# One encoder layer on one core: rows normalised before a DMA transpose, scores in f16, a new order of the steps

## The chip, the cores and the metric

One core of one Trainium2 chip runs the whole program. The metric is the device time in microseconds (us) of that core. Of the kernel before three runs are shown: 1824.67, 1825.55 and 1826.52 us, median 1825.55 us.

## The reference, cut to what matters

The layer is computed for two sequences of 1024 rows, `x_prompt` and `x_sample`, with 1024 columns each; together 16 tiles of 128 rows.

```python
h = rms_norm(x, norm1)
proj = h @ w_in                               # 512 q, 128 k, 128 v, 512 gu, 512 gv columns
q, k = rms_norm(q, q_gain), rms_norm(k, k_gain)     # per head of 64
scores = einsum("bnqkgd,bnskd->bnkgqs", qb, kband) / sqrt(64) + bias   # bands of 3 blocks of 128
probs = exp(scores - m) / (sum(exp(scores - m)) + exp(sink - m))
a = rms_norm(probs @ vband, attn_out_gain)
g = rms_norm(gelu(gu) * (w_s @ rms_norm(gelu(gv)) + b_s), gmlp_out_gain)
x = x + concatenate([a, g]) @ w_o
h2 = rms_norm(x, norm2)
x = x + (silu(h2 @ w_gate) * (h2 @ w_up)) @ w_down
```

## The kernel before, in words

**Precision.** Nearly every product is made of three f16 products: each operand is split into a high half (the value rounded to f16) and a low half (what the rounding left out), and high x high, high x low and low x high are summed in PSUM. ScalarE makes the high half, VectorE subtracts to get the low one. For the first four tiles q, k and v are formed another way, in float32r from a transposed copy of x (`x0_load`, L800; `q0`, L854; `kv_mm`, L1089), also in halves. The scores too are three float32r products before the change: `k_hi`/`k_lo` (L1170, L1178) and `q_hi`/`q_lo` (L1174, L1183) write float32r halves, and `score_mm` (L1193) multiplies them, in pairs: the two key/value heads go to the two halves of TensorE's rows (64 each), so two products run side by side, and one step is three such pairs.

**Stages.** (1) Attention stage, roughly the first 380 us of the span: input projection, band attention, the gated branch. (2) Output projection, residual, second norm, and the transposes to `h2` (`o_product`, `h2_turn`, `h2_out`, `h2_comb`, `h2_cstore`), up to about 606 us. (3) Gate, up and down products of the FFN (`matrix`, `product` at L1824 to L1826; `down_mm` at L2318 to L2320), to the end. The pieces of h2 go to DRAM (`t_d`), come back as `tr`, and are split by `top_hi` and `top_lo` (L1726).

**Who sets the order.** The steps of stages 1 and 2 are small functions, listed by `add`. A table `WHEN` (L50) holds one number for each step, and `plan_order` sorts the steps by it; they are emitted in that order under a manual schedule, so each engine's queue (TensorE, VectorE, ScalarE, GpSimd, and SyncE's queue, which issues every DMA) runs its part of the list strictly in that order, whatever is ready. The numbers are due times: successive `q0` steps of four 128x512 products stand 90 or 91 apart. What follows the list (stage 3, from the loop over `matrix` at L2330) is ordered by the framework, and can be placed among the last listed steps.

**The path that is changed.** For a tile t from 4 on: `xn_load` (L911) brings the rows in natural layout, `xn_sum` (L913) squares and sums them on ScalarE (over the tile itself), `xn_eps` and `xn_pow` (L917, L921, the latter on GpSimd) make 1/rms. `x_load` (L924) brings the same tile transposed from a second input, `xT`. Since in that layout the scale belongs to columns, `x_diag` (L928, VectorE) puts it on a diagonal, `x_row` (L931, TensorE) multiplies that by ones to have it in every row of PSUM, and `x_scale` (L935, VectorE) multiplies. `x_hi` (L938, ScalarE) and `x_lo` (L942, VectorE) split; `x_store` (L945) keeps the halves in DRAM for the gated branch, which loads them again (`x_back`). Tiles 0 to 3 go through `x_load` to `x_store` later, for the gated branch alone. `attention` lists, for each tile and pair of heads, `score_mm`, `score_out`, `score_exp`, `p_hi`, `p_lo`, `p_turn` (L1256, a DMA that transposes the f16 halves of the exponentials) and `pv_mm`; then `o_out`, `o_sq`, `o_pow`, `o_scale` (L1297, ScalarE) and `o_store`.

**Buffers.** Tiles share tagged slots: `XL` 3, `XN` 3, `S` 9, `M` 8, `L` 12. Before, `xn` (XN) is free again after `xn_sum`, `xs` (XL) after `x_lo`, and the halves of k of one sequence take two L slots.

Of the kernel before, what the change touches and what calls it, by code (L numbers as in the profile page):

```python
# [41 lines left out]
SCALE_MAX = 1e12  # L42
LATER = (4, 5, 0, 1, 2, 3)
# [3 lines left out]
WHEN = {  # L47
    "x0_load": [
        0, 18, 30, 24, 42, 36, 1108, 1278,
    ],  # L50
    "wq_load": [
        6, 12, 494, 578, 832, 939, 1024, 1700,
    ],
    "x0_hi": [
        345, 598, 768, 683, 937, 852, 2143, 2228,
    ],
    "x0_lo": [
        427, 680, 850, 765, 1019, 934, 2225, 2310,
    ],
    "wq_hi": [  # L60
        429, 514, 1044, 1128, 1570, 1974, 2059, 2505,
    ],
    "wq_lo": [
        522, 606, 1136, 1262, 1662, 2067, 2151, 2598,
    ],
    "q0": [
        522, 639, 729, 820, 910, 1111, 1228, 1319, 1409, 1553, 1643, 1760, 1851, 1941, 2032, 2122, 2213, 2303, 2394,
        2484, 2575, 2665, 2942, 3032,
    ],
    "gram": [  # L70
        612, 1202, 1500, 1526, 1734, 2756, 2782, 2809, 2835, 2849, 2862, 2875, 2889, 2902, 2915, 2928,
    ],
    "row_load": [
        325, 409,
    ],
    "row_mm": [
        1001,
    ],
    "row_out": [
        1202,  # L80
    ],
    "row_store": [
        1447,
    ],
    "wkv_load": [
        923, 917,
    ],
    "wkv_hi": [
        2567, 2607, 1890, 1930, 1761, 1801, 1841, 1720,
    ],  # L90
    "wkv_lo": [
        2664, 2703, 1961, 2001, 1832, 1872, 1913, 1792,
    ],
    "gram_sum": [
# [12 lines left out]
        3290, 7396, 22309, 25142,
    ],
    "xn_load": [
        663, 748, 1531, 1954, 1870, 5109, 5285, 7806, 8401, 11836, 13484, 15168, 16891, 18725, 20817, 22671,  # L110
    ],
    "xn_sum": [
        1298, 1467, 2402, 2841, 2656, 5538, 5714, 8258, 9243, 12848, 14151, 15992, 17664, 19714, 21744, 23515,
    ],
    "xn_eps": [
        2812, 1610, 2546, 3009, 2800, 5701, 5866, 8471, 9414, 13000, 14338, 16140, 17826, 19893, 21888, 23692,
    ],
    "xn_pow": [
        2897, 1651, 2587, 3050, 2841, 5742, 5907, 8512, 9455, 13041, 14379, 16182, 17867, 19934, 21929, 23733,
    ],  # L120
    "kv_mm": [
        3448, 3591, 3901, 4044, 3133, 3304, 4436, 4580, 6472, 6603, 7468, 7599, 9652, 9784, 10749, 10880, 13212,
        13344, 15049, 15180, 16905, 17036, 18301, 18432, 20449, 20580, 22169, 22300, 23971, 24102, 25899, 26030,
    ],
    "q_out": [
        3216, 3159, 3274, 3331, 6459, 8377, 9536, 11750, 13192, 15033, 17178, 18991, 20785, 22549, 24298, 25909,
    ],
    "v_gain": [
        3892, 4208, 3571, 3524,
    ],  # L130
    "k_out": [
        4126, 4246, 3724, 4785, 6771, 7782, 10015, 11467, 13511, 15348, 17300, 18714, 20755, 22595, 24573, 26201,
    ],
    "v_hi": [
        3938, 4456, 3749, 4760, 6785, 7767, 10164, 11105, 13526, 15362, 17225, 18600, 20770, 22732, 24344, 26276,
    ],
    "v_lo": [
        4011, 5063, 3827, 5089, 7094, 7864, 10657, 11151, 13650, 15408, 17806, 18803, 21254, 22942, 24442, 26330,
    ],
    "qk_sq": [  # L140
        4271, 4332, 4394, 5068, 6816, 8454, 10102, 11856, 13557, 15394, 17345, 19068, 20862, 22670, 24619, 26926,
    ],
# [515 lines left out]
def kernel(  # L658
# [1329 lines left out]
    def add(fn, *args):  # L1988
        steps.append((fn, args))
# [491 lines left out]
```

## Time and profile before

| what | value |
|---|---|
| median of three runs | 1825.55 us |
| the profiled execution's own time | 1824.14 us |
| span, first to last instruction | 1822.2 us (1.9 us less than its time) |
| mean granted TensorE clock | 0.996 |
| busy: TensorE, weight loads, VectorE, ScalarE, GpSimd | 1793.5, 903.5, 1179.4, 1021.3, 113.6 us |
| DMA | 306.22 MB, mean 168 GB/s |

Busy time is the union of the instructions' times. A matmul's time in the profile (379 ns for 128x512) overlaps the next one's: steady products start 216 ns apart, so what a product costs is read from starts, not from its duration. "Idle" is the time just before an instruction, with what ended it. PEclk is the granted clock. DMA share is the mean busy share of the 16 DMA engines; it can come out above 1.

### The profile page before, as it was taken

The page shows a single profiled execution, that of the slowest core. Times are in us where ns is not written, and L with a number is a line of the kernel's source. Part 1 is how long each engine was busy: PE and PEld are TensorE (multiplying, and loading weights), DVE is VectorE, ACT ScalarE, POOL GpSimd, SP SyncE. Part 2 cuts the span into 40 slices and gives each one's busy share as a digit, 9 for nine tenths or more (in the row PEclk, how much of TensorE's full clock was granted, in tenths as well). Part 3 has the DMA queues.
Part 4 walks back from the last instruction along what each step waited for, and adds up shares of the span by engine and source line. Part 5 has one row for each costly group of instructions (what it writes and reads, how often), then busy time and mean ns, then how long its engine had stood idle before and what let it go on. Part 6 is the DMA issues. An engine that isn't in the chain of part 4 may idle for free.

```text
span 1822.2 us, 26844 instructions
## 1 busy us (share of the span) xinstructions
PE 1793.5 (98%) x10070; PEld 903.5 (50%) x10070; DVE 1179.4 (65%) x2181; ACT 1021.3 (56%) x1955; POOL 113.6 (6%) x141
## 2 busy tenths in 40 slices
PE   8899999999999999999999999999999999999999
PEld 7666665555555444444444444444444444444444
DVE  5987787589688886464564564645647847554751
ACT  6987798698677955453453444534534453333340
POOL 1221110132000000000000000000000000000000
PEclk9999999999999999999999999999999999999999
DMA  7798899877699962331331322313352854233631
GB/s 251 207 215 193 206 246 271 242 256 260 211 292 318 294 223 101 110 122 68 121 125 52 116 89 97 110 70 112 120 203 93 280 182 141 91 116 104 236 134 47
DMA packets 225966, 306.22 MB, mean 168 GB/s; under 512 B 104067, under 2 KB 138883, under 8 KB 225836
## 3 DMA queue, kind: packets, MB, share of 16 engines
q1 hardware_dynamic: 225836, 304.51, 52.6%
q8 instruction: 79, 1.29, 0.3%
q14 instruction: 51, 0.42, 0.1%
HBM read 188.57 MB, written 92.82 MB: 154 GB/s over the span
## 4 chain that ended last, share of the span: by engine, by line
PE 90%; DVE 4%; DMA 3%; ACT 2%; issue 2%; POOL 0%; POOLq 0%; SPq 0%; DVEq 0%; ACTq 0%
PE pd L2318 7%; PE pd L2320 7%; PE pd L2319 7%; PE pd L1824 4%; PE pa L1824 4%; PE pd L1825 4%; PE pa L1825 4%; PE pa L1826 4%; PE pd L1826 4%; PE pc L1824 4%; PE pc L1825 4%; PE pc L1826 4%; PE ps L1202 2%; PE pb L1824 2%; PE pb L1825 2%; PE pb L1826 2%
## 5 line engine op out<-in xcount | busy, mean ns | idle before, releaser
L2318 PE MATMUL pd<-wop,a 128*128 128x512 f16 x616 | 233.5, 379 | 2.2 <-ACT a L702 2.1
L2319 PE MATMUL pd<-wop,a 128*128 128x512 f16 x616 | 233.5, 379 | 0.0
L2320 PE MATMUL pd<-wop,a 128*128 128x512 f16 x616 | 233.3, 379 | 0.0
L1825 PEld LDWEIGHTS <-op 128*128 128x128 f16 x1232 | 120.5, 98 | 148.2 <-issue 6.3
L1826 PEld LDWEIGHTS <-op 128*128 128x128 f16 x1232 | 120.5, 98 | 146.4 <-DVE op L1810 1.2
L1824 PEld LDWEIGHTS <-op 128*128 128x128 f16 x1232 | 122.2, 99 | 142.5
L1824 PE MATMUL pa<-top,op 128*128 128x512 f16 x352 | 133.4, 379 | 1.8 <-ACT ua L1942 1.8
L1826 PE MATMUL pa<-top,op 128*128 128x512 f16 x352 | 133.4, 379 | 0.7 <-DVE op L1810 0.7
L1825 PE MATMUL pa<-top,op 128*128 128x512 f16 x352 | 133.4, 379 | 0.0
L702 ACT ACTIVATE wop<-wd,wdr_r 128x512 f16<-128x512 f32 x66 | 47.3, 720 | 153.0 <-PE pd L2320 150.2
L702 ACT ACTIVATE a<-as,asr_r 128x512 f16<-128x512 f32 x154 | 102.2, 709 | 33.4 <-DMA as<-act_d 17.5
L1953 ACT COPY ub<-pc 128x512 f32<-128x512 f32 x44 | 25.8, 585 | 160.4 <-PE pc L1826 160.4
L703 DVE SCALAR_TENSOR_TENSOR wop<-wd,wdr_r,wop 128x512 f16<-128x512 f32 x66 | 49.2, 748 | 101.1 <-ACT wop L702 101.0
L703 DVE SCALAR_TENSOR_TENSOR a<-as,asr_r,a 128x512 f16<-128x512 f32 x154 | 108.9, 746 | 7.7 <-ACT a L702 7.6
L2318 PEld LDWEIGHTS <-a 128*128 128x128 f16 x616 | 60.4, 98 | 75.5 <-ACT a L702 3.2
L2320 PEld LDWEIGHTS <-a 128*128 128x128 f16 x616 | 60.2, 98 | 73.0 <-DVE a L703 0.7
L2319 PEld LDWEIGHTS <-a 128*128 128x128 f16 x616 | 60.3, 98 | 72.2
L1752 ACT ACTIVATE junk_e<-g 128x1024 f32<-128x1024 f32 x44 | 46.4, 1054 | 77.5 <-DVE g L1937 77.5
L1229 ACT ACTIVATE sc<-sc,mx 128x384 f32<-128x384 f32 (+1 forms) x128 | 74.3, 582 | 19.7 <-DVE mx L1213 17.4
L1959 DVE TENSOR_TENSOR ub<-ub,ua 128x512 f32<-128x512 f32 x44 | 30.4, 691 | 82.0 <-ACT ub L1953 82.0
L1934 ACT ACTIVATE g<-g,rs 128x512 f32<-128x512 f32 x57 | 41.1, 722 | 62.4 <-DVE g L1969 35.5
L1213 DVE CUSTOM_DVE_ANT_0 sc<-ps,bias 128x384 f32<-128x384 f32 (+1 forms) x128 | 62.9, 518 | 16.3 <-PE ps L1202 15.4
(394 smaller groups left out, 4504.3 us busy)
## 6 DMA issues: line engine op xcount, KB each, us to landing
as<-act_d SPq DMA_DIRECT2D x77, 512.0 KB, 3.4
act_d<-g SPq DMA_DIRECT2D x66, 256.0 KB, 2.0
tr<-t_d SPq DMA_DIRECT2D x28, 512.0 KB, 5.3
raw<-in_wg_dram SPq DMA_DIRECT2D x24, 512.0 KB, 3.5
raw<-in_wu_dram SPq DMA_DIRECT2D x24, 512.0 KB, 4.3
act_d<-sa SPq DMA_DIRECT2D x44, 256.0 KB, 2.4
act_d<-sb SPq DMA_DIRECT2D x44, 256.0 KB, 2.9
wds<-in_wd_dram SPq DMA_DIRECT2D x22, 512.0 KB, 3.6
```

The lines of the kernel that those rows point to most:

```text
L702: nc.scalar.mul(hi, src, gain)
L703: nc.vector.scalar_tensor_tensor(lo, src, gain, hi, ALU.mult, ALU.subtract)
L1213: nc.vector.tensor_tensor_reduce(out=T["sc", t, hp][:, v, :W], in0=T["ps", t, hp][v][:, :W], in1=bias[:, h, off : off + W], scale=1.0, sca ...
L1229: nc.scalar.activation(sc, sc, AF.Exp, bias=T["mn", t][:, h : h + 1], scale=-1.0, accum_out=T["sum", t][:, h : h + 1])
L1752: nc.scalar.activation(junk_e[0], src, AF.Square, accum_out=acc)
L1824: nc.tensor.matmul(ps, op[:, 0, k, :], th[:, k, :], start=first and k == 0, stop=False, **more)
L1825: nc.tensor.matmul(ps, op[:, 0, k, :], tl[:, k, :], start=False, stop=False, **more)
L1826: nc.tensor.matmul(ps, op[:, 1, k, :], th[:, k, :], start=False, stop=last and k == 3, **more)
L1934: nc.scalar.activation(dst, src, AF.Silu, scale=iv)
L2318: nc.tensor.matmul(ps, a[:, 0, s, cs], wop[:, 0], start=first and n == 0, stop=False, **kw)
L2319: nc.tensor.matmul(ps, a[:, 0, s, cs], wop[:, 1], start=False, stop=False, **kw)
L2320: nc.tensor.matmul(ps, a[:, 1, s, cs], wop[:, 0], start=False, stop=end, **kw)
```

## The change

1. **Rows normalised in natural layout, then transposed by DMA.** `x_diag`, `x_row`, `x_scale` and the loads of `xT` for whole tiles are gone. `x_hi` and `x_lo` scale and split the natural rows into one f16 tile (`x_quot`, an XL slot), and `x_turn`, one DMA for each tile, transposes both halves into `hT`. `xn_sum` no longer overwrites the rows of tiles from 4 on, and their XN slot is held until `x_lo`. Tiles 0 to 3 load their rows a second time (`x_load`, now of `xn`).
2. **Scores in f16.** The halves of q and k are f16, with the gains of q and k balanced between them (square root of their product, the sign on q's side), worked out once at the start by a chain of VectorE and GpSimd operations on the loaded constants; k's halves take one L slot.
3. **`o_scale`** runs on VectorE.
4. **Warm-up products.** `warm_fill` zeroes a tile on VectorE, `warm_mm` multiplies it by itself eight times on TensorE, ahead of everything.
5. **All of `WHEN` is new.** The bias row product (`row_mm`) and `gram` of the first block now stand ahead of the first `q0`.

The factor `X_NORM` moved into 1/rms, with the scalars that follow from it adapted. The diff, cut to its core:

```diff
 WHEN = {
+    "warm_fill": [
+        0,
+    ],
+    "warm_mm": [
+        62,
+    ],
     "x0_load": [
-        0, 18, 30, 24, 42, 36, 1108, 1278,
+        0, 160, 200, 320, 280, 386, 1049, 1629,
     ],
     "wq_load": [
-        6, 12, 494, 578, 832, 939, 1024, 1700,
+        40, 240, 426, 506, 580, 466, 911, 980,
     ],
...
     "q0": [
-        522, 639, 729, 820, 910, 1111, 1228, 1319, 1409, 1553, 1643, 1760, 1851, 1941, 2032, 2122, 2213, 2303, 2394,
...
+        562, 652, 743, 860, 950, 1041, 1158, 1275, 1366, 1456, 1573, 1664, 1754, 1844, 2108, 2211, 2312, 2402, 2493,
...
     "row_load": [
-        325, 409,
+        80, 120,
     ],
     "row_mm": [
-        1001,
+        425,
     ],
...
+    "x_turn": [
+        3686, 5312, 7254, 9189, 10704, 12275, 13504, 16060, 17256, 17416, 20051, 22579, 25837, 26851, 27681, 28957,
+    ],
+    "x_store": [
+        4191, 5915, 7858, 9715, 11551, 13135, 14191, 16565, 17766, 18406, 20644, 23313, 26387, 27957, 28716, 30409,
+    ],
...
     "o_product": [
...
-        57674, 57934, 58193, 58334, 58464, 58711, 58841,
...
+        56366, 56884, 57014, 56755, 57144, 57360, 57490,
     ],
...
     "top_lo": [
-        53431, 53121, 54002, 56123, 55596, 57162, 55302, 55829, 57756, 57582, 60813, 60463, 59916, 60030,
+        51626, 51800, 53008, 54739, 54410, 54296, 55009, 54014, 55801, 57035, 59126, 59413, 59882, 59239,
     ],
...
-    qg8 = cp.tile([P, 1], F32, name="qg8")
-    nc.vector.tensor_scalar_mul(qg8, qgs, -1.0 / math.sqrt(HD))
+    gains = cp.tile([P, 4], F32, name="gains")
+    qg, kg, gprod, gsign = (gains[:, n : n + 1] for n in range(4))
+    nc.vector.tensor_mul(gprod, qgs, kgs)
+    nc.vector.tensor_scalar(gsign, gprod, 0.0, -2.0, ALU.is_ge, ALU.mult)
+    nc.vector.tensor_scalar_add(gsign, gsign, 1.0)
+    nc.vector.tensor_mul(gprod, gprod, gsign)
+    nc.vector.tensor_scalar_mul(gprod, gprod, -1.0 / math.sqrt(HD))
+    nc.gpsimd.tensor_tensor(kg, gprod, pm[:, 1:2], ALU.pow)
+    nc.vector.tensor_scalar_min(kg, kg, GAIN_MAX)
+    nc.vector.tensor_mul(qg, kg, gsign)
...
+    def warm_fill():
+        T["warm"] = k4("S", "warm", (P, 512), F16)
+        nc.vector.memset(T["warm"], 0.0)
+
+    def warm_mm():
+        ps = xx("ps_warm", [P, 512])
+        for _ in range(8):
+            nc.tensor.matmul(ps, T["warm"][:, 0:P], T["warm"], start=True, stop=True)
...
-        nc.scalar.activation(xns[t], xns[t], AF.Square, scale=1.0 / 32.0, accum_out=xms[t])
+        junk = xns[t] if t < GROUP else x_quot(t).rearrange("p z d -> p (z d)").bitcast(F32)
+        nc.scalar.activation(junk, xns[t], AF.Square, scale=1.0 / 32.0, accum_out=xms[t])
...
-        xst[t] = k4("XL", f"xs{t}", (P, KD, P))
-        load(xst[t], xT[t])
-
-    def x_diag(t):
-        nc.vector.tensor_scalar(diags[t % 2], ident, rstd1[t], X_NORM, ALU.mult, ALU.mult)
-
-    def x_row(t):
-        rrow[t] = mm(f"psr{t}", [P, P])
-        nc.tensor.matmul(rrow[t], onec, diags[t % 2], start=True, stop=True)
-
-    def x_scale(t):
-        nc.vector.tensor_tensor(xst[t], xst[t], rrow[t][:, None, :].to_broadcast([P, KD, P]), ALU.mult)
+        xns[t, 1] = k4("XN", f"xm{t}")
+        load(xns[t, 1], xn[t])
+
+    def x_quot(t):
+        return lazy(("xq", t), lambda: k4("XL", f"xq{t}", (P, 2, D), F16))
 
     def x_hi(t):
+        nc.scalar.mul(x_quot(t)[:, 0], xns[t, 1] if t < GROUP else xns[t], rstd1[t])
+
+    def x_lo(t):
+        x = x_quot(t)
+        nc.vector.scalar_tensor_tensor(
+            x[:, 1], xns[t, 1] if t < GROUP else xns[t], rstd1[t], x[:, 0], ALU.mult, ALU.subtract
+        )
+
+    def x_turn(t):
         hT[t] = k4("S", f"xh{t}", (P, 2, KD, P), F16)
-        nc.scalar.copy(hT[t][:, 0], xst[t])
-
-    def x_lo(t):
-        nc.vector.tensor_sub(hT[t][:, 1], xst[t], hT[t][:, 0])
+        load(hT[t].rearrange("p z k j -> p (z k) j"), x_quot(t).rearrange("p z d -> p (z d)"), transpose=True)
...
-            kT[s] = [k4("L", f"k{c}{s}", (P, TS * P), F32R) for c in "hl"]
+            kT[s] = k4("L", f"k{s}", (P, 2, TS * P), F16)
...
-        qT[t] = k4("S", f"qt{t}", (P, 2, NH // 2, P), F32R)
-        nc.scalar.mul(qT[t][:, 0], T["pt", t], qg8)
+        qT[t] = k4("S", f"qt{t}", (P, 2, NH // 2, P), F16)
+        nc.scalar.mul(qT[t][:, 0], T["pt", t], qg)
...
-                    ps[v][:, :W], qT[t][rows, a, hp, :], kT[s][b][rows, keys], start=n == 0, stop=n == 2
+                    ps[v][:, :W], qT[t][rows, a, hp, :], kT[s][rows, b, keys], start=n == 0, stop=n == 2
...
-        nc.scalar.mul(T["o", t][:, 0], T["o", t][:, 0], T["or", t])
+        nc.vector.tensor_scalar_mul(T["o", t][:, 0], T["o", t][:, 0], T["or", t])
```

More of the change, by code (lines that the diff above doesn't have):

```diff
@@ L273 @@
+        44000,
     ],
     "o_store": [
-        11213, 10877, 12777, 15610, 15548, 18329, 19694, 20414, 22167, 24032, 26579, 27869, 30588, 35598, 35410,
-        37374,
+        10391, 10460, 12064, 13718, 16888, 16848, 20340, 20200, 22070, 23273, 24877, 27357, 28796, 33088, 33295,
+        44068,
+    ],
+    "x_hi": [
+        3403, 3670, 6931, 8840, 9948, 11601, 11904, 15776, 16973, 16000, 19186, 22123, 25528, 26560, 26878, 28585,
+    ],
+    "x_lo": [
+        3538, 3828, 7066, 9041, 10083, 11736, 12549, 15912, 17108, 16186, 19321, 22431, 25690, 26703, 27097, 28738,
+    ],
@@ new lines @@
+    "x_turn": [
+        3686, 5312, 7254, 9189, 10704, 12275, 13504, 16060, 17256, 17416, 20051, 22579, 25837, 26851, 27681, 28957,
+    ],
+    "x_store": [
+        4191, 5915, 7858, 9715, 11551, 13135, 14191, 16565, 17766, 18406, 20644, 23313, 26387, 27957, 28716, 30409,
+    ],
+    "q_mm": [
[4 rows of a table added]
+    ],
+    "g_load": [
+        3726, 4958, 4704, 4649, 6375, 7214, 5272, 7688, 19469, 22386, 21528, 21793, 23353, 24917, 25645, 25331,
+    ],
+    "g_sum": [
+        4538, 4351, 5398, 5469, 5231, 5327, 5089, 5160, 19999, 20121, 23231, 23080, 22274, 21980, 22586, 22948,
+    ],
@@ new lines @@
+    "g_hi": [
+        7276, 7474, 7756, 7621, 6869, 7142, 8306, 8188, 24607, 24716, 25344, 25406, 26266, 26131, 25805, 25984,
+    ],
+    "g_lo": [
+        7433, 8179, 8027, 7780, 6995, 7280, 8596, 8531, 24743, 24848, 25485, 25550, 26426, 26882, 26056, 26122,
+    ],
+    "gv_mm": [
[5 rows of a table added]
+    ],
+    "gv_out": [
+        9696, 11409, 13347, 15881, 17134, 18554, 20192, 22228, 23870, 26832, 27662, 26665, 28993, 29040, 29811, 32936,
+    ],
+    "gv_store": [
+        9773, 11486, 13424, 15958, 17296, 18631, 20300, 22310, 23948, 26971, 27819, 26771, 31537, 29233, 29893, 33019,
+    ],
@@ L277 @@
+    "x_back": [
+        21568, 16605, 27635, 30877, 31261, 31069, 33433, 33896, 34413, 35764, 28756, 37179, 32835, 37579, 36260,
+        39116, 38687, 39419,
     ],
     "x_load": [
[L279 to L286 removed]
@@ L335 @@
     ],
     "ws_load": [
-        20811,
+        17846,
     ],
     "vg_load": [
-        2039,
+        1560,
     ],
     "ws_sum": [
-        21581,
+        20264,
     ],
     "ws_hi": [
-        22350,
+        21224,
     ],
     "ws_lo": [
-        22524,
+        21380,
     ],
     "vg_sum": [
-        21521,
+        20367,
     ],
     "vg_add": [
-        21673,
+        20468,
     ],
     "vg_pow": [
-        21714,
+        20502,
     ],
     "vg_out": [
-        23237,
+        21123,
@@ L2001, in x_prep @@
             x_norm(t)
-        for fn in (x_load, x_diag, x_row, x_scale, x_hi, x_lo, x_store):
+        else:
+            add(x_load, t)
+        for fn in (x_hi, x_lo, x_turn, x_store):
             add(fn, t)
@@ L2053 @@
     tabs_rows()
+    add(warm_fill)
+    add(warm_mm)
     for k in range(KD):
```

388 lines of the change are left out of this document (170 added, 218 removed), and 158 rows, old and new, of the table WHEN.

## Prediction

> **What bounds the kernel now.** I read the page's busy times and chain first, then TensorE's idle time by stretch, then what ended it.
>
> ```profile
> PE 1793.5 (98%) x10070; PEld 903.5 (50%) x10070; DVE 1179.4 (65%) x2181; ACT 1021.3 (56%) x1955; POOL 113.6 (6%) x141
> PE 90%; DVE 4%; DMA 3%; ACT 2%; issue 2%; POOL 0%; POOLq 0%; SPq 0%; DVEq 0%; ACTq 0%
> ```
>
> TensorE (PE) is busy nearly throughout and carries 90% of the chain. So a part of the change counts only if it takes products away, shortens one, or removes a wait of TensorE or the slow clock behind it.
>
> ```profile
> 0.00:20.00 20.00, 14.48 (x60) 11.22 (x61) 9.55 (x17) 11.96 (x20) 2.00 (x14) 1.00 0.91 285
> ...
> 40.00:60.00 20.00, 16.59 (x101) 13.50 (x100) 19.13 (x42) 18.26 (x40) 6.98 (x4) 0.91 0.32 106
> 60.00:80.00 20.00, 16.72 (x117) 11.88 (x116) 18.25 (x56) 17.95 (x48) 4.89 (x5) 0.91 0.77 215
> ...
> 300.00:320.00 20.00, 16.40 (x119) 8.23 (x119) 12.22 (x29) 14.20 (x32) 0.55 (x1) 0.83 1.04 273
> ...
> 580.00:700.00 120.00, 113.37 (x549) 54.12 (x548) 99.93 (x148) 89.84 (x161) 4.33 (x6) 1.00 0.75 249
> 700.00:1400.00 700.00, 700.00 (x3271) 320.45 (x3270) 386.20 (x641) 313.14 (x525) 13.23 (x19) 1.00 0.30 108
> ```
>
> Second column TensorE, then weight loads, VectorE, ScalarE, GpSimd, clock, DMA share, GB/s. TensorE is idle 5.5 us at the start, 6.7 between 40 and 80, 3.6 between 300 and 320, 6.6 between 580 and 700. In two of these places the granted clock falls too, to 0.91 and 0.83. From 700 on nothing can be won, and the change does not touch it. The last stall of the attention stage, in the chain of waits:
>
> ```profile
> 297.13 8.99 DMA pT<-ph
> ...
> 306.93 0.70 ACT sc L1229 x2
> 307.64 0.94 ACT xh L940
> 308.60 2.37 DVE xh L943 x2
> ...
> 311.63 0.43 PE pgv L955
> ```
>
> A transpose of exponentials takes 9 us among full DMA queues, ScalarE and VectorE stand behind it, and products then run at 0.43 us, half speed.
>
> **The list as a measuring rod.** The due times are hundredths of a microsecond, as the trace shows: the first `q0` is due at 522, the last `o_product` at 58841.
>
> ```profile
> 5.52 2.07 PE L860 MATMUL pq<-wqt,xh_s 128*128 128x512 f32 x4 [5.52 <-ACT wqt L822]
> ...
> 604.89 0.38 PE L1601 MATMUL wd<-wo6h,mo 128*128 128x512 f16 x1
> ```
>
> They start at 5.52 and 604.89: the trace runs 0.3 us behind the list at first, 16.5 us at the end. In the new list the last `o_product` is due at 574.90 instead of 588.41, 13.5 us earlier; the last piece of h2 that the FFN waits for (`top_lo`) at 598.82 instead of 608.13, 9.3 us earlier. After the listed steps the work is the same. So the sum is: the lead of the new list, plus the difference of the two overruns. I price the parts for that.
>
> **1. The row products.** Each `x_row` was two passes, from 211.22 to the next product at 211.44:
>
> ```profile
> 211.22 0.39 PE L933 MATMUL psr<-misc,onec 128*128 128x128 f32 x2
> 211.44 0.38 PE L955 MATMUL pq<-wq,xh 128*128 128x512 f16 x1
> ...
> 212.52 0.38 PE L957 MATMUL pq<-wq,xh 128*128 128x512 f16 x1
> 212.83 0.44 PE L1202 MATMUL ps<-kh,qt 64*128 64x384 f32 x2
> 213.11 0.34 PE L1202 MATMUL ps<-kl,qt 64*128 64x384 f32 x2
> 213.28 0.34 PE L1202 MATMUL ps<-kh,qt 64*128 64x384 f32 x2
> 213.56 0.39 PE L955 MATMUL pgv<-wg,xh 128*128 128x512 f16 x1
> ```
>
> 16 x 0.22 = 3.5 us off TensorE, on the path; it is inside the list's lead, and not counted again.
>
> **2. Scores in f16.** In the same rows: L957 at 212.52 is through after 0.216, at 212.74; the next stage's product starts at 213.56. The step takes 0.82 us. Three pairs of 384 columns, at the 0.216 us that 512 columns take here, need 0.49. The excess of 0.33 has four places: 0.09 on entry, 0.12 after the first pair (0.28 where a pair needs 0.16), 0.01 after the second, 0.11 on the way out. Which are the float32r weights' and which the change to 64 rows? One more pair of rows, float32 behind f16 without a change of rows:
>
> ```profile
> 195.93 0.19 PE L1273 MATMUL po<-v,pT 128*128 128x64 f16 x1
> 195.96 0.63 PE L1168 MATMUL pt<-ident,qk 128*128 128x128 f32 x4
> ```
>
> Nothing extra: 0.03 us, as between its f16 neighbours. So entry and exit go with the rows, and stay; what f16 can take is the 0.12 + 0.01. I take 0.13 saved, 0.20 left, for each of 52 entries (54 in the new list; adjacent steps share one). Bounds: nothing saved, or all but the 0.05 that the new list allows. Below nothing is excluded: the second pair streams at the f16 rate already, so f16 has nothing to lose there. The Trainium skill, "TensorEngine Tiling", Key Properties, has the rule behind the entry and exit: a change of tiling mode drains TensorE. By it 0.13 is all there is to win; were it wrong here, the upper bound would hold, which is a rival below.
>
> The lists allow 0.02 over the streaming time before, 0.05 after (smallest spacings behind a 384-wide step: 51 and 54). So the scores overrun their list by 0.31 x 52 = 16 us before, and 0.15 x 54 = 8 after.
>
> **3. The start.** The first four products took 2.07 us (the row at 5.52), later ones 0.24 each:
>
> ```profile
> 9.91 1.08 PE L860 MATMUL pq<-wqt,xl_s 128*128 128x512 f32 x4
> ...
> 1.19 2.84 DMA xs_s<-in_xT_dram
> ...
> 12.81 0.95 PE ps_row L880 x2
> ...
> 18.09 0.84 PE gram L870 x8
> 18.93 1.91 PE pq L860 x8
> ...
> 2.48 0.15 DVE L726 TENSOR_SCALAR qg<-cst 128x1 f32<-128x1 f32 x1 [2.48 <-DMA cst<-in_consts_dram]
> ...
> L922 POOL TENSOR_TENSOR rstd_all<-x_e,nhalf 128x1 f32<-128x1 f32 x16 | 9.3, 585 | 70.7 <-DVE x_e L919 70.6
> ```
>
> The third `q0` step, due at 729, starts at 9.91: overrun 2.6, of which 2.3 came in these ten us. Eight products on zeros can remove it, if they are over before the data come. Now the row product stands ahead of the first `q0`: its loads are third and fourth in SyncE's queue, issued by about 2.5 us, land about 2.8 later like the first load here, 5.3, then 0.95 for the product and 0.45 for `gram`: 6.7, where the list has 562. Overrun 1.1. The other bound is that the zeroing waits on VectorE behind the new gains chain (the constants land at 2.5; eight operations of 0.15, a GpSimd power of 0.6 and the zeroing: 4.5), then 8 x 0.43 on the slow clock, then 1.4: first `q0` at 9.6, overrun 4. I take the first, since the zeroing needs nothing of the chain. `gram` overruns both lists alike (0.105 a product in the row, 0.066 in the list, x48: 1.9 us).
>
> **4. x by DMA.** On VectorE and ScalarE:
>
> ```profile
> L936 DVE TENSOR_TENSOR xs<-xs,psr 128x1024 f32<-128x1024 f32 x16 | 19.5, 1218 | 13.1 <-PE psr L933 13.0
> L1298 ACT ACTIVATE o<-o,a_r 128x512 f32<-128x512 f32 x16 | 11.3, 717 | 0.6 <-POOL a_r L1295 0.6
> L1390 DVE TENSOR_SCALAR gm<-gm,misc 128x512 f32<-128x512 f32 x16 | 7.7, 482 | 0.7 <-POOL misc L1387 0.7
> ```
>
> VectorE loses 19.5 (and the diagonals), gains 16 x 0.48 for `o_scale` by the like row L1390; ScalarE loses 11.3. None of it is on TensorE's path; it thins the waits that the list holds, so it is in the lead. What is new is a wait on SyncE's queue: `x_turn` waits for VectorE's `x_lo`, and `x_store` behind it for the transpose to land. Rows for a transpose of 12 blocks, against the plain load it replaces:
>
> ```profile
> L1260 SPq DMA_TRANSPOSE pT<-ph x50: 1231/1592/4856, 82.6 to 302.7; - x50
> ...
> pT<-ph SPq DMA_TRANSPOSE x64, 4.1
> ...
> xs<-in_xT_dram SPq DMA_DIRECT2D x16, 512.0 KB, 5.0
> ```
>
> `x_turn` has 16 blocks: 2.1 us of issue, 5.5 to land. The list puts `x_store` 5.05 after `x_turn` at the closest (3686, 4191), so SyncE can stand 0 to 0.5 us at each of 16, more when queues are full, and the exponentials' transposes, loads and stores queued behind it wait as long; VectorE's and TensorE's next steps wait for those. Between 0 and 16 x 0.5 = 8 us; the list leaves the first product 6.1 us after `x_turn` or more, which covers most. I take 1.5. The stall at 306 I leave as it is (some 4 us of overrun, slow clock included): the same queues are as full.
>
> **The sum.** Overruns before: 0.3 + 2.3 (start), 1.9 (gram), 16 (scores), 4 (stall) = 24.5, of which the trace shows 16.5: idle time in the list took up a third. After: 1.1 + 1.9 + 8 + 4 + 1.5 = 16.5; the new list has less idle time there (13 us against 22, counting its gaps between TensorE's steps up to 400 us), so I let it take up a quarter: 12. Difference 4.5. Lead: between 9.3 and 13.5. Stage 3's first products fill gaps, but VectorE is at 100 of 120 us there, so 10. Together 14.5 off the profiled 1824.14, 1809.6; the median stands 1.4 above that execution: 1811.
>
> **The rivals.**
> *Scores shed their whole excess* (the entry and exit were the weights' after all). Overrun of the scores 0 instead of 8, three quarters of it felt: 6 more, 1805. For: the first pair's 0.12 shows that such weights cost. Against: the two rows at 195.9.
> *Scores and list give less*: f16 takes nothing off (overrun 0.28 x 54 = 15, so 5 more felt) and the tail binds at its 9.3: 1817. That would be a change that does not do what it says. For: the exit and entry rows. Against: 0.28 after a pair that needs 0.16.
> *The start comes late* (point 3's other bound): 2 to 3 more, 1814.
> *The DMA engines become the bound*, and it is slower:
>
> ```profile
> 500.00:520.00 20.00, 20.00 (x112) 11.22 (x110) 19.45 (x35) 16.25 (x37) 1.49 (x3) 1.00 0.98 328
> 280.00:300.00 20.00, 20.00 (x172) 11.42 (x171) 16.32 (x36) 17.55 (x39) 2.51 (x2) 1.00 1.09 272
> 82.00:310.00 228.00, 224.90 (x2061) 139.71 (x2059) 185.26 (x473) 190.20 (x449) 36.46 (x35) 1.00 0.93 225
> ```
>
> Without transposes (500 to 520) a full share moves 335 GB/s. From 82 to 310, 212 us of share moved 51 MB; 50 transposes of about 0.37 MB are 18 of them, the other 33 take 99 us at 335, so the transposes took 113: an estimate of 160 GB/s, 3.3 us for an `x_turn`, 1.6 for a plain load. 16 turns less 16 loads plus 4 reloads: 53 - 25 + 6 = 34 us, some 28 in this window: 240 in 228. If a share of 1 is a wall, the stage grows by 12 instead of shrinking, and only some 4 us from the ends are kept: 1833. It decides from a share of 1 through the whole stage. For: the 9 us transpose at 297. Against: 280 to 300 ran at 1.09 with TensorE busy throughout. The Trainium skill, "Advanced Engine Details and Errata", X-Bar Transpose, says that transposing DMAs on trn2 are as fast as regular ones; by that the addition would be the reloads' 6 us and this rival would fall, but the estimate from the rows says half the rate, and I go by it.
>
> **How the numbers follow.** Forecast 0.55 (1811, alone 1804 to 1818); whole excess 0.15 (1805); less 0.13 (1817); late start 0.05 (1814); DMA-bound 0.12 (1833, from 1822 to 1840). The range 1800 to 1823 leaves out nearly all of the last and a little below. 0.2%, 3.7 us, is what can be told from no change: faster 0.84, same 0.06, slower 0.10.
>
> **What would show it.** Right: no L933; score steps of about 0.69 us with entry and exit unchanged; `q0` at 0.23 us from its first, near 6.7; the last `o_product` near 588 and stage 3 as long as before; clock drops no more than now. Wrong: score steps near 0.54 (first rival) or 0.82; the first `q0` after 9; SyncE waiting long at `x_store`, transposes landing in 6 us and more, TensorE idle between 80 and 300, a share above 1 there (last rival); more idle time in 580 to 700 than 6.6 us would mean that the lead is lost at the seam.

## The result, and the profile after

The changed kernel takes 1836.45 us (median of four runs, 1832.6 to 1839.06), beside 1825.11 for the kernel before: a ratio of 1.0064, interval 1.0043 to 1.0085, 12 us slower. The forecast was 14.5 us faster. The profiled execution took 1832.6 us, the lowest of the four. Each later run has its ratio to runs of the kernel before that were made beside it; 0.001 is 1.8 us.

From the page of the changed kernel, the busy times and the chain:

```profile
PE 1789.8 (98%) x10046; PEld 881.4 (48%) x10046; DVE 1168.2 (64%) x2172; ACT 1020.9 (56%) x1945; POOL 116.4 (6%) x142
PE 74%; DMA 9%; ACT 7%; DVE 6%; issue 3%; SPq 1%; POOL 0%; POOLq 0%; ACTq 0%; DVEq 0%
```

TensorE is busy 3.7 us less, in a span 8.6 us longer (1830.8): its idle time went from 28.7 to 41.0 us. It carries 74% of the chain in place of 90%; DMA, ScalarE and VectorE took that over. Where, say the windows (columns as in the prediction), first of the changed kernel:

```profile
0.00:20.00 20.00, 16.97 (x59) 10.95 (x60) 10.49 (x23) 10.00 (x15) 2.00 (x14) 1.00 0.82 261
60.00:80.00 20.00, 18.45 (x161) 11.61 (x160) 17.90 (x57) 19.16 (x49) 3.96 (x3) 1.00 0.82 186
80.00:100.00 20.00, 15.92 (x124) 8.51 (x123) 16.31 (x42) 15.35 (x37) 2.51 (x2) 0.83 0.95 194
80.00:310.00 230.00, 217.68 (x2016) 121.49 (x2015) 173.83 (x463) 185.67 (x444) 37.37 (x35) 0.99 1.02 225
320.00:380.00 60.00, 51.81 (x504) 27.36 (x503) 32.09 (x85) 48.88 (x102) 8.75 (x15) 0.94 1.05 297
580.00:700.00 120.00, 112.02 (x545) 53.83 (x543) 102.78 (x147) 86.07 (x155) 3.49 (x4) 1.00 0.76 253
```

and of the kernel before:

```profile
80.00:310.00 230.00, 226.90 (x2078) 141.31 (x2075) 187.26 (x477) 191.92 (x455) 36.46 (x35) 1.00 0.93 226
320.00:380.00 60.00, 59.94 (x562) 33.06 (x561) 34.67 (x88) 44.75 (x102) 9.69 (x15) 1.00 0.90 263
```

Up to 80 TensorE idles less than before (3.0 us in the first row in place of 5.5, 1.6 in the second in place of 3.3). From 80 to 310 TensorE now idles 12.3 us in place of 3.1, and from 320 to 380, where nothing was lost before, 8.2, at a mean clock of 0.94. The first place where it is lost, in the chain:

```profile
70.36 5.93 DMA pT<-ph
...
79.04 7.88 DMA xh<-xq
...
86.97 0.61 PE pq L969
```

and in SyncE's queue:

```profile
70.36 7.55 SPq L1274 DMA_TRANSPOSE pT<-ph  x3
...
79.04 3.60 SPq L957 DMA_TRANSPOSE xh<-xq  x1
```

Three transposes of exponentials hold the queue for 7.55 us, `x_turn` (L957) then for 3.6, and its tile lands 7.9 us after its issue. The list gives 6.1 between `x_turn` and the first product (7254, 7862). TensorE waits 1.4 us for it, and what follows runs at 0.43 us a product, half speed, until 91.4. But a longer wait, for VectorE, stands ahead of that one, and e1 below, which copies in place of transposing, has both waits and the same clock. First TensorE's row of the changed kernel, then that of e1 and its window:

```profile
84.08 0.32 PE L1216 MATMUL ps<-k,qt 64*128 64x384 f16 x1 [2.50 <-DVE mx L1227]
```

```profile
84.23 0.32 PE L1216 MATMUL ps<-k,qt 64*128 64x384 f16 x1 [3.01 <-DVE mx L1227]
```

```profile
80.00:100.00 20.00, 16.10 (x117) 8.71 (x114) 16.89 (x42) 15.69 (x37) 2.51 (x2) 0.83 0.87 197
```

So this place belongs to the new order, with or without transposes. All transposes together (duration minimum, median, maximum in ns), and the median from issue to landing:

```profile
L1274 SPq DMA_TRANSPOSE pT<-ph x64: 1232/1742/4020, 66.7 to 364.8; - x64
L957 SPq DMA_TRANSPOSE xh<-xq x16: 1740/3617/6326, 43.1 to 323.2; - x16
...
pT<-ph SPq DMA_TRANSPOSE x64, 5.3
xh<-xq SPq DMA_TRANSPOSE x16, 6.1
```

The second place has two parts. TensorE idles 5.4 us of the 8.2 before 340, and the chain there goes through SyncE's queue: `x_turn`, a transpose of exponentials, and a store that ScalarE waits for:

```profile
320.00:340.00 20.00, 14.59 (x103) 6.60 (x102) 7.82 (x24) 9.22 (x19) 0.00 (x0) 0.85 1.06 255
```

```profile
324.78 2.44 SPq L957
327.27 1.50 SPq L1274
...
328.86 2.96 DMA gv_d<-gr
```

In e1, without the transposing `x_turn`, TensorE idles 0.8 us from 320 to 340. From 340 on the chain is ScalarE's:

```profile
348.57 1.28 ACT L1384
...
349.86 0.69 ACT gm L1384
...
351.69 1.28 ACT L1253
...
354.32 1.28 ACT L1384
...
356.32 1.28 ACT L1243
...
361.07 1.28 ACT L1384
```

Each 1.28 without a tile's name is the load of a function table: L1384 is gelu, L1243 and L1253 are exponentials. The new order puts five gelus, in four places, among the last exponentials; tables are loaded 11 times in place of 5, seven of them between 339 and 361 us (an expectation below counts eight). TensorE is busy throughout from 340 to 360; it waits right behind the last load, at full clock:

```profile
363.10 0.38 PE L969 MATMUL pgu<-wg,xb 128*128 128x512 f16 x1 [2.78 <-ACT gm L1384]
```

The start and a pair of score steps on the same timeline:

```profile
1.19 3.60 PE L812 MATMUL ps_warm<-warm 128*128 128x512 f16 x8 [1.19 <-DVE warm L807]
6.63 1.86 PE L894 MATMUL ps_row<-misc,tabs 33*8 33x512 f32 x2 [1.84 <-DMA misc<-in_onehot_dram]
8.42 1.11 PE L884 MATMUL gram<-wqt 128*128 128x128 f32 x4
9.33 3.72 PE L874 MATMUL pq<-wqt,xh_s 128*128 128x512 f32 x8
...
94.88 0.38 PE L971 MATMUL pq<-wq,xh 128*128 128x512 f16 x1
95.19 1.15 PE L1216 MATMUL ps<-k,qt 64*128 64x384 f16 x12
96.27 0.20 PE L1285 MATMUL po<-v,pT 128*128 128x64 f16 x1
```

The first `q0` starts at 9.33, and eight products take 3.5 us: the clock is slow in spite of the warm-up. The two score steps take 1.17 us (94.88 + 0.216 to 96.27); six pairs need 0.98, which leaves 0.19 for one entry and one exit, close to the 0.20 predicted.

Against its list the trace is behind by 7.8 us at a due time of 25 us (before: 3.6), 11.0 at 100 (4.0), 20.8 at 200 (10.1), 29.2 at 300 (17.9) and 36.0 at the last `o_product` (16.5), which starts at 610.90 in place of 604.89. From there to the end of the span it is 1219.9 us in place of 1217.3.

### The profile page after: what moved, and what is told of

The parts are those of the page before. It is cut to its first block, busy times and chain, and to the rows that moved or that the text cites. A ratio compares the mean times of both kernels' runs of the same rounds, so it can differ in the third digit from the quotient of the medians.

```text
span 1830.8 us, 26772 instructions
## 1 busy us (share of the span) xinstructions
PE 1789.8 (98%) x10046; PEld 881.4 (48%) x10046; DVE 1168.2 (64%) x2172; ACT 1020.9 (56%) x1945; POOL 116.4 (6%) x142
## 3 DMA queue, kind: packets, MB, share of 16 engines
q8 instruction: 78, 1.28, 0.3%
## 4 chain that ended last, share of the span: by engine, by line
PE 74%; DMA 9%; ACT 7%; DVE 6%; issue 3%; SPq 1%; POOL 0%; POOLq 0%; ACTq 0%; DVEq 0%
PE pd L2336 7%; PE pd L2337 7%; PE pd L2338 7%; PE pa L1838 4%; PE pa L1840 4%; PE pa L1839 4%; PE pd L1838 4%; PE pd L1840 4%; PE pd L1839 4%; PE pc L1840 4%; PE pc L1838 4%; PE pc L1839 4%; DMA pT<-ph 3%; PE pb L1838 2%; PE pb L1839 2%
## 5 line engine op out<-in xcount | busy, mean ns | idle before, releaser
L1243 ACT ACTIVATE sc<-sc,mx 128x384 f32<-128x384 f32 (+1 forms) x128 | 74.2, 581 | 16.3 <-DVE mx L1227 15.7
L1268 DVE TENSOR_TENSOR ph<-sc,ph 128x768 f16<-128x768 f32 (+1 forms) x64 | 56.4, 886 | 22.8 <-ACT ph L1263 22.6
```

The costliest lines, as they stand in the source:

```text
L1243: nc.scalar.activation(sc, sc, AF.Exp, bias=T["mn", t][:, h : h + 1], scale=-1.0, accum_out=T["sum", t][:, h : h + 1])
L1268: nc.vector.tensor_sub(ph[:, 1], T["sc", t, hp][:, :, :W], ph[:, 0])
```

## The experiments

| run | base, and its edit | median us | ratio to before, interval |
|---|---|---|---|
| e1 | changed: `x_turn` a plain copy | 1822.43 | 0.9987, 0.9977 to 0.9998 |
| e2 | before: 16 more transposes | 1865.65 | 1.0223, 1.0205 to 1.0242 |
| e3 | before: scores in f16 | 1820.44 | 0.9974, 0.9960 to 0.9988 |
| e4 | changed: row product later | 1837.74 | 1.0077, 1.0055 to 1.0100 |
| e5 | changed: plain copy in 256-byte pieces | 1829.92 | 1.0019, 1.0005 to 1.0033 |
| e6 | e3 and eight warm-up products | 1816.45 | 0.9948, 0.9931 to 0.9965 |
| e7 | changed: x chain 3 us earlier | 1848.10 | 1.0109, 1.0082 to 1.0137 |
| e8 | changed: stores from GpSimd's queue | 1845.81 | 1.0113, 1.0088 to 1.0138 |
| e9 | e4, `gram` later, 11 warm-up products | 1837.89 | 1.0069, 1.0055 to 1.0084 |
| e10 | e5 and eight tiny loads per tile | 1853.96 | 1.0158, 1.0142 to 1.0174 |
| e11 | e6 with six warm-up products | 1818.97 | 0.9959, 0.9947 to 0.9971 |
| e12 | e6, `o_scale` on VectorE, row product later | 1819.34 | 0.9960, 0.9948 to 0.9972 |
| e13 | e9, row product later still | 1837.31 | 1.0068, 1.0055 to 1.0082 |
| e14 | e13 and `x_turn` a plain copy | 1822.37 | 0.9991, 0.9976 to 1.0007 |
| e15 | e6, 11 warm-up products, row product later | 1815.74 | 0.9957, 0.9944 to 0.9969 |
| e16 | changed: Square for Gelu | 1831.35 | 1.0044, 1.0032 to 1.0057 |
| e17 | e14 and Square for Gelu | 1816.43 | 0.9956, 0.9943 to 0.9968 |
| e18 | before: Square for Gelu | 1824.31 | 1.0005, 0.9995 to 1.0014 |

The theory after the result was that the sixteen added transposes cost the time, by their packets or by the time for which they hold SyncE. The rival: the new order itself, with margins too thin, whatever the transposes.

### Transposes: e1, e2, e5, e10, e7, e8

```diff
# e1
-        load(hT[t].rearrange("p z k j -> p (z k) j"), x_quot(t).rearrange("p z d -> p (z d)"), transpose=True)
+        load(hT[t].rearrange("p z k j -> p (z k j)"), x_quot(t).rearrange("p z d -> p (z d)"))
# e2, in the kernel before, in x_lo
+        load(
+            xst[t].rearrange("p k j -> p (k j)").bitcast(F16).rearrange("p (n j) -> p n j", j=P),
+            hT[t].rearrange("p z k j -> p (z k j)"),
+            transpose=True,
+        )
```

> The changed kernel with one edit: x_turn copies the same bytes without transposing them (so the products get rows in the wrong layout; the transposition is left out of the computation). Order, waits, buffers and issue points stay. If the sixteen transposes are what costs (as transfers or as issue time on SyncE), the overrun of the last o_product falls from 36 us to about 20 and the time from 1836 to 1816 to 1824 us. If the new order, with its thinner margins, is at fault, it stays within 4 us of 1836.

> The kernel before with one addition: behind each x_lo a transposing DMA of the same size as x_turn, from the finished halves into the dead x tile; nobody reads it. If such transposes cost by themselves, whatever the order, it is slower by 12 to 20 us (1837 to 1845). If the old order has room for them and the new order is at fault, it is slower by less than 4 us.

e1: 14 us less than the changed kernel. The transposes cost that, as expected. The overrun at the last `o_product` did not show it in the profiled execution, which was e1's slowest (1829.58): 33.5 us in place of the 20 expected; e14 has 25.2. By these two traces the loss comes behind 100: at that due time e1 and the changed kernel are both 11 us behind, at 300 they are 21.6 and 29.2. e2 went the same way, but by 41 us, over twice the most expected. It adds transposes without taking the loads away, and each waits for `x_lo` in SyncE's queue; how much of the 41 us is that wait was not separated.

```diff
# e5: 16 pieces of 256 bytes for each partition, overlapping at the source
+        x = x_quot(t)
+        x = bass.AP(tensor=x.tensor, offset=x.offset, ap=[x.ap[0], [112, 16], [1, P]])
+        load(hT[t].rearrange("p z k j -> p (z k) j"), x)
# e10: e5, and behind it
+        for n in range(8):
+            load(tiny[:, 8 * n : 8 * n + 8], consts[0:1, 0:8])
```

> The changed kernel with x_turn as a plain copy in pieces of 256 bytes (as many packets, and as many bytes, as the transposing DMA moves, but no transposing; the transposition is left out, and the pieces overlap at their source, so the products get wrong numbers). If the DMA engines' time for so many small packets is the price, the time is that of the changed kernel, 1832 to 1840. If the price is the transposing instruction itself (SyncE's issue time of 3.6 us in place of 0.5, with all that is queued behind it), it is near the plain copy's 1822.

> The run with x_turn as a plain copy in small pieces, and behind each of the sixteen copies eight loads of 32 bytes on SyncE's queue, read by nobody: some 3 us of issue time each time, as the transposing form takes, with almost nothing for the DMA engines to move. If the time for which x_turn holds SyncE is what the transposing form costs beyond its packets, this brings the 8 us back: 1835 to 1840. If not, it stays at 1828 to 1832, and the remainder belongs to the transfer itself.

The issue of e5's copy on SyncE, its landing, and the window:

```profile
L959 SPq DMA_DIRECT2D xh<-xq x16: 599/621/1248, 43.1 to 316.9; - x16
...
xh<-xq SPq DMA_DIRECT2D x16, 512.0 KB, 6.1
...
80.00:310.00 230.00, 222.91 (x2059) 125.53 (x2057) 178.48 (x474) 190.86 (x455) 38.94 (x37) 1.00 1.02 233
```

The changed kernel's packets, DMA share (1.02) and landing time (6.1 us) are all there, but SyncE is held 0.62 us, not 3.62. TensorE idles 7.1 us in this window, not 12.3; the time lies between e1 and the changed kernel. And e10:

```profile
L962 SPq DMA_DIRECT2D tiny<-in_consts_dram x128: 212/246/6438, 43.9 to 350.3; - x128
...
80.00:310.00 230.00, 207.64 (x1908) 116.11 (x1907) 167.71 (x444) 174.18 (x420) 35.87 (x34) 0.98 0.92 207
```

Loads of 32 bytes, with nothing to move: the DMA share falls to 0.92, TensorE idles 22.4 us, and the kernel is 25 us slower than e5. Added up over the trace's rows from 80 to 310, issuing holds SyncE 135 us before, 151 in e1, 172 in e5, 181 in the changed kernel, 185 in e10 (45 of them the tiny loads). So what stands in SyncE's queue can cost without moving bytes, and a share of 1 is no wall. But the issue time that these sums count is not the whole of it: 25 us is three times the 8 expected, and e10 is 17 us slower than the changed kernel with about the same sum. One tiny load took 6.4 us to issue, and eight of them waited 7.2 us for the copy ahead. So e10 does not show that the transposing form costs by its issue time alone. Of the transposes' 14 us some 8 go with the transposing form (changed kernel less e5) and some 6 with the packets (e5 less e1). That split is rough: the intervals of e1 and e5 leave 3 to 9 for the packets, and in the two profiled executions e5 is only 1 us further behind its list than e1 at 300 (22.6 against 21.6).

Where do the transposes reach TensorE? Its waits, in us in total, times and the longest, with them (e13, the changed kernel with its start mended) and without (e14, the same with a plain copy):

```profile
PE po L1275 <- DMA pT<-ph: 9.5, 9, 1.3
PE ps L1206 <- DVE mx L1217: 8.1, 5, 3.4
```

```profile
PE ps L1206 <- DVE mx L1217: 4.1, 4, 3.1
...
PE po L1275 <- DMA pT<-ph: 2.3, 2, 1.4
```

`po` waits for the transposes of exponentials, `ps` for VectorE's work on earlier scores. TensorE's wait for `x_turn` itself is 0.5 us in e13, 2.8 in the changed kernel: the loss comes by what stands behind it in the queue. SyncE's own wait for the transposes to land, at `x_store`, is small too (changed kernel, whole span):

```profile
SPq L960 <- DMA xh<-xq: 4.2, 4, 2.1
```

> The changed kernel with the chain of each tile from 6 on (xn_load to x_turn) listed 3 us earlier; the first products of the tile stay where they are. If the loss is that the list leaves too little time for a transpose to land (6 us against 7.9 measured for tile 6), most stalls and slow-clock stretches between 80 and 330 go, and the time falls by 8 us or more, to 1828 or below. If SyncE's queue or the DMA engines lack capacity, the same work comes as late as before: within 4 us of the changed kernel.

> The changed kernel with x_store, o_store and gv_store issued from GpSimd's queue instead of SyncE's (23 us of SyncE's issue time between 80 and 310, and its waits for the transposes to land, go; the DMA traffic is the same, and GpSimd's powers now queue behind the stores). If SyncE's queue is the bound: 8 us or more less than the changed kernel, 1828 or below. If the DMA engines are: within 4 us of it, or slower where powers come late.

Both theories that asked for less failed here. e7 is 8 us slower than the changed kernel, though its transposes landed sooner (5.1 us for x, 4.9 for the exponentials). TensorE's waits of e7 (columns as above):

```profile
PE ps L1202 <- DVE mx L1213: 11.9, 13, 3.7
PE po L1271 <- DMA pT<-ph: 8.4, 8, 2.3
```

The first was 7.1 in five waits: with the x chain listed ahead, the scores' work on VectorE comes later, and the next scores wait for it. The list has no 3 us to move. In e8 the stores land later from GpSimd's queue (5.3 us for `x_store` against 3.6), and the gated branch waits for them:

```profile
PE po L1285 <- DMA pT<-ph: 11.8, 10, 2.4
PE pgu L969 <- DMA xb<-xh_d: 7.2, 3, 4.4
```

The transposes held SyncE no less for it (medians 1.85 and 3.73 us). e8 replaces one delay by another, so it decides nothing on SyncE. Putting `x_turn` on another queue was not tried.

### Scores and warm-up in the old order: e3, e6, e11, e12, e15

```diff
# e3, with the changed kernel's chain of gains
-            kT[s] = [k4("L", f"k{c}{s}", (P, TS * P), F32R) for c in "hl"]
+            kT[s] = [k4("L", f"k{c}{s}", (P, TS * P), F16) for c in "hl"]
-        qT[t] = k4("S", f"qt{t}", (P, 2, NH // 2, P), F32R)
+        qT[t] = k4("S", f"qt{t}", (P, 2, NH // 2, P), F16)
# e6: e3, and
+    add(warm_fill)
+    add(warm_mm)
# e11 and e15: e6, and range(6), range(11)
-        for _ in range(8):
+        for _ in range(6):
# e12 and e15: e6, and
-    "row_mm": [1001],  "row_out": [1202],  "row_store": [1447],
+    "row_mm": [1290],  "row_out": [1430],  "row_store": [1560],
# e12 also
-        nc.scalar.mul(T["o", t][:, 0], T["o", t][:, 0], T["or", t])
+        nc.vector.tensor_scalar_mul(T["o", t][:, 0], T["o", t][:, 0], T["or", t])
```

> The kernel before, in its own order, with the scores in f16 alone (halves of q and k in f16, gains balanced; k keeps its two slots). By the prediction each of 52 steps is 0.13 us shorter, 6.8 us on TensorE, of which three quarters are felt: about 1820 us. If the waits of the stage take it all back, 1825. Should its time be above 1825, the score edit itself would be part of the loss.

> The kernel before in its own order with the scores in f16 and the eight warm-up products ahead, but with row product, loads and x path as before. By the prediction's point 3 the start's 2.3 us of slow clock go, of which two thirds or more are felt: 1.5 to 2.5 us under the 1820 of the scores alone. If TensorE sits idle too long between the warm-up and the first q0 (the changed kernel showed half clock there in spite of it), the start is as before: 1820.

> The kernel before with f16 scores and six warm-up products in place of eight: TensorE is idle 0.87 us longer ahead of the first q0 (1.7 in place of 0.8). If an idle time of that length gives the faster clock up, the first products run at 0.45 us each for some 4 us, and the time goes back to that of the scores alone, 1820. If it is the number of warm-up products that counts, less of it; if neither, 1816.5.

> The kernel before in its own order, with f16 scores and eight warm-up products, o_scale on VectorE as in the change, and the row product listed 3 us later, so that TensorE does not wait for its loads (1.0 us at 10.9). No x path by DMA, no new order. 1 us less than the 1816.5 with scores and warm-up, 1815.5; o_scale by itself nothing, since neither ScalarE nor VectorE ends the waits there. If VectorE, which has more to do now, comes late: 1817 to 1820.

> The kernel before in its own order, with f16 scores, eleven warm-up products (the last ends when the first data are there, so no idle time is left) and the row product 3 us later. Every run then keeps the clock at the start: 1815 to 1816, with less spread than with an idle time of 1.6 us (1816.0 to 1819.6). If the eleven delay the first q0: 1817.

e3 gains 4.7 us, as expected. e6 gains another 4.7 by its ratio and beats both kernels; by its overrun at the last `o_product` (10.1 us, e3 12.6) it is 2.5, nearer to the 2 expected. The first product after the warm-up, in e6, e11 and e12:

```profile
5.58 1.19 PE L879 MATMUL pq<-wqt,xh_s 128*128 128x512 f32 x4 [0.80 <-ACT wqt L841]
```

```profile
5.55 2.08 PE L879 MATMUL pq<-wqt,xh_s 128*128 128x512 f32 x4 [1.62 <-ACT wqt L841]
```

```profile
5.98 1.19 PE L873 MATMUL pq<-wqt,xh_s 128*128 128x512 f32 x4 [1.58 <-ACT wqt L835]
```

After 0.80 us of idle time four products take 1.19 us, after 1.62 they take 2.08, as without any warm-up, and e11's overrun at the end is e3's (12.8 us). Whether the idle time did it is open: e12 ran at the full clock after 1.58, behind eight warm-up products. In e11 the six start some 0.43 us apart, so the full clock may never have been reached. In time the four kernels with warm-up cannot be told apart (0.9948 to 0.9960, overlapping). The six runs of e11 fall into two of 1815.6 and 1816.2 and four of 1818.7 to 1820.2; e12's profiled execution took 1816.01, its other four 2.6 to 3.6 us more. A clock kept in some executions and lost in others would fit that, but only one of each is profiled, and e15, which fills the gap with eleven products but for 0.53 us, has the spread too (1815.19 to 1818.99), against what was expected. That `o_scale` costs or gains anything does not show.

### The start in the new order: e4, e9, e13, e14

```diff
# e4
-    "row_load": [80, 120],  "row_mm": [425],  "row_out": [572],  "row_store": [736],
+    "row_load": [325, 409],  "row_mm": [855],  "row_out": [1000],  "row_store": [1150],
# e9: e4, and the first entry of gram
-        536, 834, 1132, 1248, 1546, 1935, 1962, 1988, 2014, 2028, 2041, 2054, 2068, 2081, 2094, 2198,
+        612, 834, 1132, 1248, 1546, 1935, 1962, 1988, 2014, 2028, 2041, 2054, 2068, 2081, 2094, 2198,
-        for _ in range(8):
+        for _ in range(11):
# e13: e9, and (e14 has e1's plain copy too)
-    "row_mm": [855],  "row_out": [1000],  "row_store": [1150],
+    "row_mm": [1250],  "row_out": [1300],  "row_store": [1370],
```

> The changed kernel with the bias row product behind the first q0 steps again (row_load at 325 and 409, row_mm at 855, row_out and row_store 4 us later). First q0 near 6.5 us in place of 9.3, with the faster clock of the warm-up products. If the start's loss is carried to the end: 3 to 4 us less than the changed kernel, 1833. If what comes later sets the end of the stage anyway: the same time as the changed kernel.

> The changed kernel with its start mended: row product later (as in the run with the row later), gram of the first block behind the first q0, and eleven warm-up products in place of eight, so that the last one ends near 6 us, when the first data are there. If the slow clock at the start needs an idle time of more than about 1.5 us (1.70 and 1.84 brought it, 0.80 did not), all q0 steps run at 0.23 us a product and 4 to 5 us are gained at 25 us; carried through, 1831. If the stage's end is set by its transfers alone, the same time as the changed kernel, 1836.

> The changed kernel with its start mended in full: as in the run with the start mended, and the row product at 1250, where it no longer waits for its loads (1.57 us of idle time there had brought the slow clock back). Overrun at 25 us near 3 in place of 7.8. If what is gained at the start is carried to the end: 1831 to 1832. If transfers and SyncE set the end of the stage by themselves, and TensorE only waits longer later: 1835 to 1838.

> The same start, and x_turn as a plain copy of large pieces (the transposition is left out, so the products get rows in the wrong layout). With the transposes gone there is slack, and the start's gain is carried: 1822.4 less 4 to 5, about 1818, no better than the order of before with scores and warm-up (1816.5). If the list's lead of 9 to 13 us is real once start and transposes are out of its way: 1811 or below. If not even the start is carried, 1822.

e4 has its first `q0` at 6.58, but behind the third product at half speed: `gram` ahead of it had waited 1.70 us. In e9 the wait came later:

```profile
11.46 1.02 PE L884 MATMUL ps_row<-misc,tabs 33*8 33x512 f32 x2 [1.57 <-DMA misc<-in_onehot_dram]
```

and eight products then took 2.9 us, the first three still fast. e13 has no such wait, its overrun at 25 us is 4.9 in place of 7.8, and its time is that of the changed kernel. e14 is that of e1. So in the new order the start is not carried, with or without transposes; later waits swallow it. In the old order it was carried: e6 is 1.7 us ahead of e3 against their common list at 25 us, 2.5 at the end.

### The table loads: e16, e17, e18

```diff
-        nc.scalar.activation(y, y, AF.Gelu_apprx_tanh, scale=cgu[:, 0:1])
+        nc.scalar.activation(y, y, AF.Square, scale=cgu[:, 0:1])
```

and likewise for the gelu of `gu_out`.

> The changed kernel with Square in place of Gelu on ScalarE (gelu is left out of the computation; the instructions stay, but no table is loaded for them). The new order puts gelus among the exponentials and loads a table 11 times instead of 5, eight of them between 339 and 361 us, where ScalarE is busy 19.7 of 20 us. If these loads delay the path, it is 5 us or more faster than the changed kernel, 1831 or below; the control (the kernel before, edited alike) gains less than 2. If ScalarE only looks full there: within 2 us.

> The changed kernel with the start mended in full, x_turn as a plain copy and Square in place of Gelu (the transposition and gelu are left out). If transposes, start and table loads are all that ails the new order, 1822 less 5 to 8: 1814 to 1817, as the old order with scores and warm-up. If its lead is there once they are gone: 1811 or below. If something else holds it: 1820 and above.

> Control: the kernel before with Square in place of Gelu (gelu is left out). Three table loads of 1.28 us fewer, one of them among the last exponentials at 360 us: 0 to 2 us faster than the kernel before.

e18 gains nothing: the old order's loads cost no time. e16's ratio is 0.0020 under the changed kernel's and 0.0024 under e13's, 4 us, somewhat less than expected and hardly clear of the noise: the intervals overlap. In its trace TensorE idles 6.5 us from 320 to 340, so that part of the second place is not the loads', and 0.5 in place of 2.8 from 360 to 380. Without transposes the gain is clear: e17 is 6.4 us under e14. The window from 320 to 380, in e14 and e17:

```profile
320.00:380.00 60.00, 54.57 (x517) 29.19 (x516) 40.10 (x104) 56.75 (x117) 11.04 (x19) 0.97 0.88 268
```

```profile
320.00:380.00 60.00, 58.72 (x563) 31.44 (x562) 43.84 (x112) 52.45 (x123) 13.99 (x22) 1.00 0.99 295
```

ScalarE is at 56.75 of 60 us in e14; without the loads TensorE wins 4.2 us back there, and the full clock. e17 stands where e15 stands, within their intervals.

## Why the prediction was wrong

Read as a ladder of ratios: the old order with scores and warm-up, 0.9957 (e15); the new order freed of transposes and table loads, the same (e17, 0.9956); table loads put in, 0.9991 (e14); transposes put in, 1.0068 (e13); the changed start in place of the mended one, no difference (1.0064). So:

1. **Point 4 is the main step that failed.** "I take 1.5", from a bound of 0 to 8 us, for what `x_turn` does to SyncE and the transfers; it is 14 (e13 less e14). The bound priced one wait, SyncE's at `x_store` until the transpose lands, and that wait is 4.2 us in all. The time for which `x_turn` itself holds SyncE was estimated and then given no term in the sum. It is 3.6 us each, where 2.1 was estimated by the number of blocks, and 58 us for all sixteen, added up over the trace's rows, where the loads of `xT` that they replace took 8. (12 blocks still take 1.74 in the same kernel, so the time does not go by blocks, and why was not found.) "The list leaves the first product 6.1 us after `x_turn` or more, which covers most" looks at the wrong wait: TensorE's for `x_turn` itself is 0.5 to 2.8 us. The path that the prediction named, the exponentials' transposes behind it and what waits for those, is where most of the loss shows (e13 beside e14).
2. **The DMA-bound rival** had the time, 1833, and the signs named for it came: landing in 6 us, TensorE idle between 80 and 300, a share above 1. The one sign that failed was SyncE waiting long at `x_store`. But its mechanism, a wall at a share of 1, is not what the runs show: e5 bears the same share at 1.0019, and e10 is slower at 0.92. The packets cost some 6 us, and the transposing form some 8 beyond them; that SyncE's held queue is what costs there is argued, not shown by itself. Its estimate of half the rate is borne out by the packets: 256 bytes take 25 ns on a DMA engine and 4096 bytes 197 on average (changed kernel, 80 to 310), so a tile takes 3.2 us of the sixteen engines in 2048 small pieces and 1.6 in 128 large ones. The Trainium skill's rule that was weighed there ("Advanced Engine Details and Errata", X-Bar Transpose) holds only against a copy cut into the same pieces: 6.1 us to land in both, with a copy in large pieces at 5.2.
3. **The lead of 10 us was not there.** It was read from the due times of two lists as if both were kept alike. e17 reaches its last `o_product` at 594.0, e15 at 597.8: 3.8 us of 13.5 are left, since e17 is 19.1 us behind its list there, e15 9.4. And these are given back after it: 1220.7 us to the end against 1215.6. In the changed kernel the sign named for that is there too: TensorE idles 8.0 us from 580 to 700 in place of 6.6. The bound by `top_lo`, 9.3, was the one to take: less the 9.7 us by which e17 is further behind its list, it leaves nothing. That overruns are felt less in a list with less idle time was seen ("a quarter" for "a third"), but by far too little. Which waits make up the rest of e17's overrun was not separated.
4. **The table loads were not looked for.** "All of `WHEN` is new" was priced by spacings on TensorE. The kinds of functions on ScalarE, in order, would have shown gelus among the exponentials. They cost 6.4 us without the transposes (e14 less e17); with them, 4 by e16, hardly clear of the noise.
5. **The scores were right**: 0.13 us a step, entry and exit kept. The step predicted at 0.69 takes 0.69 in the 13 places where it stands alone behind a 128x512 product with no wait, and e3 gained 4.7 us where 5 were to be felt.
6. **The start** came late, as the rival had it (9.3 against its 9.6), but not by VectorE's chain: the zeroing was done at 1.19, the row product waited for its second load until 6.63, and the products behind that wait ran at half clock. Whether the wait lost the full clock or the eight warm-up products, 0.43 us apart, had not reached it does not show. Mended, it would have changed nothing in this order. Row products (point 1) are gone from the trace; by themselves they were not tried.

The sum by the same ladder: 1825.1, less 7.8 for scores and warm-up (e15), nothing for the rest of the new order (e17), 6.4 for the table loads, 14.1 for the transposes: 1837.8, where 1836.45 was measured. The forecast differs from it mainly by the lead of 10, by the transposes' 14 taken as 1.5, and by the table loads.

## What to carry to other kernels

Before pricing a new order by its planned end, check each queue's order for what the plan may not price: how long each DMA holds its issuing queue and what stands behind it, and switches of function on ScalarE. A margin between a DMA and its first reader is not enough; what is queued behind the DMA needs one too. A stall in the changed kernel is not yet the work of the part that one suspects: the first one here was in e1 as well. The old order with three small edits, scores in f16, warm-up products that last nearly until the first data come, and the row product later (e15), beats the kernel before by 0.4% and the changed one by 1.1%.

## What the runs showed of the hardware

- **The length of an idle time alone does not decide on the clock.** At the start, 1.57 us (e9) and 1.70 (e4) lost it: what came behind ran at full speed for some 1.2 us (e4) and 1.9 (e9), then at half for some 3. 1.58 (e12) kept it. Later in the changed kernel 2.78 us at 363 kept it, as the row above shows; 2.50 at 84, with 1.42 behind it, did not. The Trainium skill, "TensorE: Matmul & The Clock Gate", What's actually happening, gives an idle window of about 3.4 us that runs free of the kernel. A free-running window fits that equal idle times went different ways; that 1.57 us was enough does not fit its length, and here the rows decide.
- **A transposing DMA holds its queue** six times as long as a plain one with the same pieces (3.62 against 0.62 us), though both land after 6.1 (medians of sixteen, changed kernel and e5).
- **Sixteen times eight loads of 32 bytes cost 25 us** when they stand in a queue that others wait behind (e10 beside e5).
